# Decoder layer with a routed mixer: last expert's down products in one row, token ranks read with a selection mark, first expert's partial sums outside its weight slot

## The chip, the cores and the metric

The kernel runs on one core of one Trainium2 chip. The metric is device time of one execution in microseconds (us), from the first to the last instruction and what the runtime puts around them. Before the change the median of 3 runs is 339.26 us (338.2 to 341.36).

## What is computed

One decoder layer for 256 tokens of width 1024, all in float32. First come two attention groups (four heads of differential attention, eight heads of block-sparse attention) with one input and one output projection. Then follows a mixture of experts, and it alone is touched by the change:

```python
g_logits = t @ router_group                      # 256 tokens x 4 groups
g = argmax(g_logits)                             # one group for each token
e_logits = (t @ router_expert[g])                # 8 experts in that group
top_v, top_e = top_k(e_logits, 2)                # two experts for each token
weight = softmax(g_logits)[g] * softmax(top_v)
...
hid = silu(xc @ w_gate[e]) * (xc @ w_up[e])      # for each of 32 experts, hidden width 256
out = hid @ w_down[e]
y[token] += out * weight
```

Each expert has three weight matrices of 1 MB (w_gate, w_up, w_down), so the 32 experts read 96 MB, and the two projections 16 MB.

## The kernel before

**Stages.** The attention part fills the first 125 us or so. Then the residual is added, the router's logits are made (`routed`), and `select(c)` picks two experts for each token of the 128-token half c (c = 0, 1). The tokens of an expert get places in a slot table of 32 places (CAP): `select` multiplies the one-hot choices `oh` by the strict triangle `tri` (and by `ones` for the earlier half), which gives in PSUM, for every expert, how many chosen tokens stand before this one (`prk`). Two VectorE instructions (L569, L570) turn it into `R1`: the rank plus 1 where the token chose the expert, else 0. `places(g, c)` (L601) compares R1 with the numbers 1 to 32 (`iota1`) for the four experts of group g, which gives the gather matrix `Pm`, and scales it by the token's norm (`Ps`). Eight matmuls a half (L871) gather the tokens of the first four experts into `pgs`, `gathered` (L612) writes them to `xe`, and the experts begin.

**An expert.** `gate(e)` and `up(e)` (L668) multiply the expert's 32 gathered tokens by its weights, in 8 matmuls each, which lie in four column strips of the array and run four at a time (each is recorded as two passes, so 16 records). The results are partial sums over four strips. ScalarE (L678) and VectorE (L683) copy them to SBUF: **into the first 512 columns of the expert's own gate weight slot**, which is not read any more by then. One expert later `folded` (L688) transposes them on TensorE, adds the four strips, and makes the hidden values `hT`. Another expert later `down` (L706) multiplies by w_down. The outputs of four experts are gathered in `oG` and brought back to the tokens by `combine` (L741). For the last 8 experts each has its own way back: `moved` (L725, L726) copies the product from PSUM, and `spread` (L731) adds it to the tokens in 8 matmuls.

**Weights.** Units of 1 MB are loaded in the fixed order of their use, all on the queue of SyncE (SP), into 23 slots: 16 of a ring, others that open as earlier buffers end, and x2's place. Units 16 and 17 are w_gate and w_up of expert 0; the experts' units follow. `fill` issues a unit's transfer when its slot's last reader is done; the transfer waits for that reader's semaphore, and for the transfer eight issues earlier (eight completion semaphores in rotation). The ring's first refill by an expert's slot is unit 39 (w_up of expert 8), then 40 (w_down of expert 6) and 41. The last unit, 111 (w_down of expert 31), goes in pieces (`CUTS`): contraction half 0 whole (512 KB), half 1 in two pieces of 256 KB.

**Order.** TensorE runs the experts' matmuls in program order (`pe`). The places touched are `select`, `places`, `gate`, `weighted` (which allocated oG of the first group), the lines after the first expert, and the end: down(30), spread(29), half 0 of down(31), spread(30), two `warmed` matmuls (128x512 of zeros, whose result nobody reads), half 1 of down(31), and `last`: moved(31), spread(31), the copies to `res` and the output transfers.

Of the kernel before, what the change touches and what calls it, by code (L numbers as in the profile page):

```python
# [9 lines left out]
F32 = mybir.dt.float32  # L10
F32R = mybir.dt.float32r
BF16 = mybir.dt.bfloat16
# [3 lines left out]
ALU = mybir.AluOpType  # L16
# [19 lines left out]
LATE3_AT = 16 + SLOTS - 1  # L36
CUTS = ((0, 0, 1024), (1, 0, 512), (1, 512, 1024))
OVER_E, OVER_N = 12, 4
ROWS_Q = 4

A_COLS = {}
# [10 lines left out]
def hybrid_layer_kernel(ctx: ExitStack, tc: tile.TileContext, x, xt, w_in, w_out, w_gate, w_up, w_down, smalls, relb, out):  # L52
# [496 lines left out]
    def select(c):  # L549
        pl, d = pls[c], sel[c]  # L550
        gm, gi, pen = small("gm", 8), small("gi", 8, U32, xr), small("pen", 4, F32, xr)
        Lm, em, ei = small("Lm", E, F32, None, "t32", 3), small("em", 8), small("ei", 8, U32, xr)
        oh, mb = small("oh", 2 * E, BF16).rearrange("p (i e) -> p i e", i=2), small("mb", E, F32, None, "t32", 3)
        nc.vector.max(gm, pl[:, 32:40])
        nc.vector.max_index(gi, gm, pl[:, 32:40])
        nc.vector.tensor_tensor(pen, gi[:, 0:1].broadcast_to([P, 4]), col("iota")[:, 0:4], op=ALU.not_equal)
        nc.vector.scalar_tensor_tensor(
            Lm.rearrange("p (g e) -> p g e", g=4), pen.unsqueeze(2).broadcast_to([P, 4, 8]), -1.0e30,
            pl[:, 0:32].rearrange("p (g e) -> p g e", g=4), op0=ALU.mult, op1=ALU.add)
        nc.vector.max(em, Lm)  # L560
        nc.vector.max_index(ei, em, Lm)
        nc.vector.tensor_tensor(oh, ei[:, 0:2].unsqueeze(2).broadcast_to([P, 2, E]),
                                col("iota").unsqueeze(1).broadcast_to([P, 2, E]), op=ALU.is_equal)
        d["oh"] = oh
        prk = pl[:, 64 : 64 + E]
        in_order(*[lambda c2=c2, i=i: nc.tensor.matmul(
            prk, tri if c2 == c else ones, sel[c2]["oh"][:, i, :], start=c2 == 0 and i == 0, stop=c2 == c and i == 1)
            for c2 in range(c + 1) for i in range(2)])
        nc.vector.tensor_tensor(mb, oh[:, 0, :], oh[:, 1, :], op=ALU.add)  # L569
        nc.vector.scalar_tensor_tensor(R1[:, c, :], prk, 1.0, mb, op0=ALU.add, op1=ALU.mult)  # L570
        d.update(gm=gm, em=em)

# [29 lines left out]
    def places(g, c):  # L602
        p = ew.tile([P, G, CAP], F32, name="Pm", tag="Pm", bufs=2)
        r = R1[:, c, g * G : (g + 1) * G].unsqueeze(2).broadcast_to([P, G, CAP])
        it = col("iota1").unsqueeze(1).broadcast_to([P, G, CAP])
        nc.vector.tensor_tensor(p, r, it, op=ALU.is_equal)
        ps_ = ew.tile([P, G * CAP], F32, name="Ps", tag="Ps", bufs=2)
        state["ps"] = nc.vector.tensor_scalar(ps_, p.rearrange("p g s -> p (g s)"), rstd[:, c : c + 1], None, op0=ALU.mult)
        return p, ps_
# [35 lines left out]
    def weighted(st):  # L645
# [7 lines left out]
        st["pT"] = ex.tile([P, S], F32, name="pT", tag="pT")  # L653
        st["o"] = ex.tile([P, D], F32, name="oG", tag="oG")
        nc.scalar.activation(st["pT"], pt[:, :S], AF.Copy)
# [19 lines left out]
    def gate(e, st):  # L675
        t, pg = half(e, st, 0, place[e - 1][0] if e else None)
        st["parts"] = t
        nc.scalar.activation(*paired(t[:, :HID], pg), AF.Copy)  # L678
        return t
# [67 lines left out]

    def last(hT, dv, pd):
        res = spare("res").rearrange("p (c n) -> p c n", c=NC)
        for nh in range(2):  # L750
            down_product(hT, dv, pd, (1,), (2 * nh, 2 * nh + 1))
        moved(2 * G - 1, pd)
# [11 lines left out]
    def overflow():  # L764
        rv = nc.values_load(flag[0:1, 0:1], min_val=0, max_val=S)
        used["ring"] += [over_at - 1] * OVER_N
        with tc.If(rv > CAP):  # L767
# [20 lines left out]
            for c in range(NC):  # L788
                nc.vector.scalar_tensor_tensor(wo[:, c, :], R1[:, c, :], CAP + 0.5, W[:, c, :], op0=ALU.is_gt, op1=ALU.mult)
            with tc.For_i(0, E, 1) as ie:  # L790
# [64 lines left out]
    in_order(opened[0], *routed(1, 512, xTa), *turnb, opened[1])  # L855
    squared(1, 512, 256, ppa, 1)
    select(0)
    in_order(*routed(1, 768, xTb))
    squared(1, 768, 256, ppb, 2)
    pools["x2"] = x2.rearrange("p c n -> p (c n)")  # L860
# [23 lines left out]
    with tc.issue_after(state["ps"].ins):  # L884
        for c in range(NC):
            weights(c)
    pc = pls[1][:, 128 : 128 + E]
# [9 lines left out]
    for e in range(1, E):  # L897
# [37 lines left out]
        if 0 <= e - OVER_E - 1 < 2 * G:  # L935
            residual(*divmod(e - OVER_E - 1, G))
    down(*queue.pop(0), place[E - 1][0])
    spread(done.pop())
    dv = unit(place[E - 1][2]).rearrange("p (c n) -> p c n", c=2)
    pd = ps.tile([P, 512], F32, name="pd", tag="tr")  # L940
    down_product(hT, dv, pd, (0,), range(4))
    spread(2 * G - 2)
    warmed(2, "pp")
    last(hT, dv, pd)

# [18 lines left out]
def _layout(inputs):  # L964
# [8 lines left out]
    def rows(v):  # L973
# [11 lines left out]
        "g2p": a["norm2_g"][0].reshape(P, KC),  # L985
        "tri": (idx[:, None] < idx[None, :]).astype(np.float32),
        "iota": rows(np.arange(E, dtype=np.float32)),
        "iota1": rows(np.arange(1, CAP + 1, dtype=np.float32)),
        "router": np.concatenate(
# [29 lines left out]
```

## Time and profile before

| | us |
|---|---|
| median of 3 runs (lowest to highest) | 339.26 (338.2 to 341.36) |
| the profiled execution's own time | 340.07 |
| its span, first to last instruction | 337.8 |
| TensorE busy in the span | 317.0 (94%) |
| VectorE busy | 193.9 (57%) |
| ScalarE busy | 138.5 (41%) |
| GpSimd busy | 12.0 (4%) |
| mean granted clock of TensorE, of full speed | 0.98 |
| bytes moved | 123.20 MB, mean 365 GB/s |

Times within the span start at its first instruction. PE is TensorE's matmuls, PEld its weight loads, DVE VectorE, ACT ScalarE, POOL GpSimd, SP SyncE, whose only work is to issue transfers. A busy share is an average over stages with different limits. The granted clock is a share of 2.4 GHz: 1.00 is that level and 0.50 is 1.2 GHz. Some records of matmuls and of landings are missing.

### The profile page before, as it was taken

How to read it: one execution, taken by the hardware profiler on the slowest of the kernel's cores; microseconds unless marked ns; L12 is line 12 of the kernel's file. 1: busy time of each engine (PE TensorE's matmuls, PEld its weight loads, DVE VectorE, ACT ScalarE, POOL GpSimd, SP SyncE). 2: the span in 40 equal slices, each digit the busy share in tenths (PEclk: the TensorE clock that was granted, in tenths of full speed). 3: DMA queues.
4: the chain of work that ended last, by engine and by line, in shares of the span. 5: the costliest groups of instructions: out<-in, count | busy, mean ns of one | idle time of the engine just before them, and what ended most of it. 6: DMA issues, size and time to landing. Idle time of an engine off the chain costs nothing. (4 is left out here: it accounts for less than half of the span.)

```text
span 337.8 us, 7426 instructions
## 1 busy us (share of the span) xinstructions
PE 317.0 (94%) x2858; PEld 213.6 (63%) x2858; DVE 193.9 (57%) x601; ACT 138.5 (41%) x362; POOL 12.0 (4%) x20
## 2 busy tenths in 40 slices
PE   8889999999999998999999939999999999999971
PEld 4658877788777788575676714664665675575430
DVE  2767858878998657756454532355354466333302
ACT  4875667958786434324222221213213224212101
POOL 0100001000120131000000000000000000000000
PEclk9999999999999999999999996999999999999978
DMA  7999999999725896899999999999999999999923
GB/s 213 397 385 288 390 387 396 414 414 420 253 84 199 314 422 253 321 422 419 423 419 419 418 425 418 419 421 418 422 422 422 420 419 419 419 422 418 415 94 124
DMA packets 25544, 123.20 MB, mean 365 GB/s; under 512 B 2311, under 2 KB 3380, under 8 KB 13348
## 3 DMA queue, kind: packets, MB, share of 16 engines
q1 hardware_dynamic: 24772, 120.91, 89.4%
q0 software_dynamic: 304, 1.02, 1.0%
q10 hardware_dynamic: 432, 0.79, 0.7%
q8 instruction: 24, 0.39, 0.5%
q14 instruction: 12, 0.10, 0.1%
HBM read 121.64 MB, written 1.07 MB: 363 GB/s over the span
## 5 line engine op out<-in xcount | busy, mean ns | idle before, releaser
L668 PE MATMUL pgu<-u,xe 128*32 128x256 f32 x992 | 67.7, 391 | 6.4 <-PEq L767 5.5
L256 PE MATMUL pp<-hi,xh 128*128 128x512 f32 (+1 forms) x132 | 53.3, 405 | 2.2 <-ACT hi L245 2.2
L246 DVE TENSOR_TENSOR lo<-u,hi 128x512 fp32r<-128x512 f32 x63 | 43.1, 702 | 16.0 <-ACT hi L245 15.9
L256 PE MATMUL pp<-lo,xh 128*128 128x512 f32 (+1 forms) x132 | 51.5, 393 | 0.0
L256 PE MATMUL pp<-hi,xl 128*128 128x512 f32 (+1 forms) x132 | 51.5, 390 | 0.0
L668 PEld LDWEIGHTS pgu<-u,xe 128*32 128x32 f32 x992 | 28.9, 111 | 34.2 <-issue 13.2
L245 ACT ACTIVATE hi<-u 128x512 fp32r<-128x512 f32 x64 | 39.0, 626 | 19.0 <-PE pp L256 13.3
L720 ACT ACTIVATE oG<-pd 32x256 f32<-32x256 f32 x48 | 17.9, 374 | 56.9 <-PE pd L706 45.2
L706 PE MATMUL pd<-u,hT 128*32 128x256 f32 x496 | 34.0, 391 | 2.6 <-DMA u<-in_w_down_dram 2.4
L722 DVE COPY oG<-pd 32x256 f32<-32x256 f32 x48 | 20.3, 423 | 27.0 <-ACT oG L720 25.2
L256 PEld LDWEIGHTS pp<-hi,xh 128*128 128x128 f32 x132 | 25.0, 189 | 9.5 <-ACT hi L245 3.8
L256 PEld LDWEIGHTS pp<-lo,xh 128*128 128x128 f32 x132 | 24.8, 188 | 6.6 <-DVE rv L153 0.6
L256 PEld LDWEIGHTS pp<-hi,xl 128*128 128x128 f32 x132 | 24.9, 188 | 4.6
L624 PEld LDWEIGHTS pg<-Ps,x2q 128*128 128x128 f32 x224 | 25.5, 192 | 2.9 <-DVE gu L691 1.6
L624 PE MATMUL pg<-Ps,x2q 128*128 128x128 f32 x224 | 26.9, 278 | 0.0
L691 DVE TENSOR_REDUCE gu<-ptr 128x64 f32<-128x256 f32 x32 | 13.6, 425 | 21.2 <-PE ptr L688 20.8
L683 DVE COPY u<-pgu 128x256 f32<-128x256 f32 x31 | 13.2, 424 | 21.4 <-PE pgu L668 21.4
L706 PEld LDWEIGHTS pd<-u,hT 128*32 128x32 f32 x496 | 14.2, 111 | 15.1 <-issue 6.0
L741 PE MATMUL y<-oG,pT 128*128 128x256 f32 x96 | 21.7, 379 | 0.0
L688 PEld LDWEIGHTS ptr<-sm,u 128*128 128x128 f32 x124 | 13.3, 143 | 13.1 <-issue 10.2
L688 PE MATMUL ptr<-sm,u 128*128 128x128 f32 x124 | 20.8, 291 | 0.0
L678 ACT ACTIVATE u<-pgu 128x256 f32<-128x256 f32 x31 | 11.9, 383 | 20.4 <-PE pgu L668 19.3
(168 smaller groups left out, 359.9 us busy)
## 6 DMA issues: line engine op xcount, KB each, us to landing
u<-in_w_gate_dram SPq DMA_DIRECT2D x31, 1024.0 KB, 19.5
u<-in_w_up_dram SPq DMA_DIRECT2D x31, 1024.0 KB, 19.8
u<-in_w_down_dram SPq DMA_DIRECT2D x30, 1024.0 KB, 19.7
u<-in_w_in_dram SPq DMA_DIRECT2D x11, 1024.0 KB, 12.5
u<-in_w_out_dram SPq DMA_DIRECT2D x4, 1024.0 KB, 14.7
x<-in_x_dram SPq DMA_DIRECT2D x2, 512.0 KB, 10.9
x<-in_w_gate_dram SPq DMA_DIRECT2D x1, 1024.0 KB, 8.8
x<-in_w_down_dram SPq DMA_DIRECT2D x1, 1024.0 KB, 19.8
```

The costliest lines, as they stand in the source:

```text
L245: nc.scalar.activation(hi, raw, AF.Copy)
L246: (nc.gpsimd if u * 4 + k == 3 else nc.vector).tensor_tensor(lo, raw, hi.bitcast(F32), op=ALU.subtract)
L256: yield lambda a=a, w=w, kk=kk, i=i: nc.tensor.matmul(pp, a, w[:, cols], start=first and kk == 0 and i == 0, stop=last and kk == len(hls) ...
L624: pe(nc.tensor.matmul(pg[:, j * P : (j + 1) * P], x2q[:, c, q4 * 4 + j, :], st["P"][c][1], start=c == 0, stop=c == NC - 1))
L668: pe(nc.tensor.matmul(pg[q * CAP : (q + 1) * CAP, :HID], st["xe"][:, k, j0 : j0 + CAP], wv[:, k, :], start=r == 0, stop=r == KC // ROWS_Q ...
L683: nc.vector.tensor_copy(*paired(t[:, HID : 2 * HID], pg))
L688: pe(nc.tensor.transpose(pt[:, j * P : (j + 1) * P], t[:, j * P : (j + 1) * P], ident))
L691: nc.vector.tensor_reduce(gu[:, :2], parts[:, :2], axis=AX.X, op=ALU.add)
L706: pe(nc.tensor.matmul(pd[j * 32 : (j + 1) * 32, :256], hT[:, c, :], dv[:, c, j * 256 : (j + 1) * 256], start=c == 0, stop=c == 1, tile_pos ...
L720: nc.scalar.activation(dst, pd[j * 32 : (j + 1) * 32, :256], AF.Copy)
L722: nc.vector.tensor_copy(dst, pd[j * 32 : (j + 1) * 32, :256])
L741: pe(nc.tensor.matmul(y[j][:, c * 256 : c * 256 + 256], st["pT"][:, c * P : (c + 1) * P], st["o"][:, j * 256 : (j + 1) * 256], start=st["g ...
```

## The change

The change makes these edits.

- The triangle gets 512 (`SEL`) on its diagonal, so the product itself holds the rank plus 512 where the token chose the expert, and `iota1` runs from 512 to 543. The first group's places read this product in PSUM; the two instructions that made R1 are gone from `select`, and R1, which later groups use, is copied from PSUM after the first group's places, ahead of `weights`.
- Expert 0's partial sums go to oG, which is allocated at gate(0) now; `weighted` allocates it for later groups alone.
- At the end spread(29) and six `warmed` matmuls come ahead of down(30), all 8 products of down(31) follow down(30) directly, then spread(30) and `last`. The last unit's half 1 is one piece of 512 KB.
- `squared` stands two lines later in the source.

```diff
-CUTS = ((0, 0, 1024), (1, 0, 512), (1, 512, 1024))
+CUTS = ((0, 0, 1024), (1, 0, 1024))
...
+SEL = 512
...
-        nc.vector.tensor_tensor(mb, oh[:, 0, :], oh[:, 1, :], op=ALU.add)
-        nc.vector.scalar_tensor_tensor(R1[:, c, :], prk, 1.0, mb, op0=ALU.add, op1=ALU.mult)
-        d.update(gm=gm, em=em)
+        d.update(gm=gm, em=em, rank=prk)
...
-        r = R1[:, c, g * G : (g + 1) * G].unsqueeze(2).broadcast_to([P, G, CAP])
+        r = (R1[:, c] if g else sel[c]["rank"])[:, g * G : (g + 1) * G].unsqueeze(2).broadcast_to([P, G, CAP])
...
-        st["o"] = ex.tile([P, D], F32, name="oG", tag="oG")
+        if g:
+            st["o"] = ex.tile([P, D], F32, name="oG", tag="oG")
...
         t, pg = half(e, st, 0, place[e - 1][0] if e else None)
-        st["parts"] = t
+        if e == 0:
+            t = st["o"] = ex.tile([P, D], F32, name="oG", tag="oG")
...
-    def last(hT, dv, pd):
+    def last(pd):
         res = spare("res").rearrange("p (c n) -> p c n", c=NC)
-        for nh in range(2):
-            down_product(hT, dv, pd, (1,), (2 * nh, 2 * nh + 1))
         moved(2 * G - 1, pd)
...
-    squared(1, 512, 256, ppa, 1)
     select(0)
     in_order(*routed(1, 768, xTb))
+    squared(1, 512, 256, ppa, 1)
...
         for c in range(NC):
+            nc.vector.tensor_copy(R1[:, c, :], sel[c]["rank"])
             weights(c)
...
+    spread(done.pop())
+    warmed(6, "pp")
     down(*queue.pop(0), place[E - 1][0])
-    spread(done.pop())
     dv = unit(place[E - 1][2]).rearrange("p (c n) -> p c n", c=2)
     pd = ps.tile([P, 512], F32, name="pd", tag="tr")
-    down_product(hT, dv, pd, (0,), range(4))
+    down_product(hT, dv, pd, range(2), range(4))
     spread(2 * G - 2)
-    warmed(2, "pp")
-    last(hT, dv, pd)
+    last(pd)
...
-        "tri": (idx[:, None] < idx[None, :]).astype(np.float32),
+        "tri": (idx[:, None] < idx[None, :]).astype(np.float32) + SEL * np.eye(P, dtype=np.float32),
...
-        "iota1": rows(np.arange(1, CAP + 1, dtype=np.float32)),
+        "iota1": rows(np.arange(SEL, SEL + CAP, dtype=np.float32)),
```

In the built program the order of instructions moves at three places.

On VectorE, at the choice for the second half of the tokens, before. oh is the one-hot choice, mb and R_1581 (R1) are the two that go, pl is the PSUM bank with the rank:

```order
L561 MAX_INDEX ei<-em,Lm 128x8
L562 TENSOR_TENSOR oh<-ei,sm 128x64
L569 TENSOR_TENSOR mb<-oh 128x32
L570 SCALAR_TENSOR_TENSOR R_1581<-pl,mb 128x32
L606 TENSOR_TENSOR Pm<-R_1581,sm 128x128
L608 TENSOR_SCALAR Ps<-Pm,rstd 128x128
L586 SCALAR_TENSOR_TENSOR ngm<-gm,rstd 128x1
```

And after:

```order
L562 MAX_INDEX ei<-em,Lm 128x8
L563 TENSOR_TENSOR oh<-ei,sm 128x64
L605 TENSOR_TENSOR Pm<-pl,sm 128x128
L607 TENSOR_SCALAR Ps<-Pm,rstd 128x128
L885 COPY R_1581<-pl 128x32
L585 SCALAR_TENSOR_TENSOR ngm<-gm,rstd 128x1
L586 SCALAR_TENSOR_TENSOR ngm<-em,rstd 128x1
L885 COPY R_1581<-pl 128x32
```

Pm follows oh directly and reads PSUM, and two copies stand behind Ps. ScalarE's instructions stand in the same order before and after, so the moved `squared` moves nothing.

On SP's queue, at the first refills of the experts' slots, before. u_1784 is unit 39, u_1786 unit 40, u_1819 unit 41; in brackets stand the semaphores that each waits for (DMAHW: a transfer's completion):

```order
L140 DMA x_64<-in_w_gate_dram 128x2048 [waits PE_49,DMAHW5_49,Activation_49,Pool_49]
L140 DMA u_1784<-in_w_up_dram 128x2048 [waits DMAHW6_49,PE_49]
L140 DMA u_1786<-in_w_down_dram 128x2048 [waits DVE_49,DMAHW7_49,PE_49,Activation_49]
L140 DMA u_1819<-in_w_gate_dram 128x2048 [waits DMAHW0_49,PE_49]
L140 DMA u_1821<-in_w_up_dram 128x2048 [waits DVE_49,DMAHW1_49,PE_49,Activation_49]
```

And after (u_1781, u_1783, u_1816 and u_1818 are the same units 39 to 42):

```order
L141 DMA x_64<-in_w_gate_dram 128x2048 [waits PE_49,DMAHW5_49,Activation_49,Pool_49]
L141 DMA u_1781<-in_w_up_dram 128x2048 [waits DMAHW6_49,PE_49]
L141 DMA u_1783<-in_w_down_dram 128x2048 [waits DMAHW7_49,PE_49]
L141 DMA u_1816<-in_w_gate_dram 128x2048 [waits DMAHW0_49,PE_49]
L141 DMA u_1818<-in_w_up_dram 128x2048 [waits DVE_49,DMAHW1_49,PE_49,Activation_49]
```

The order is the same, the waits are not: unit 39 took the slot of unit 17 before and waited for the last matmul of up(0); it takes the slot of unit 16 now and waits for the last matmul of gate(0). Unit 40 took the slot of unit 16 and waited for the transposes of folded(0); it takes the slot of unit 17 now and waits for up(0).

On TensorE, at the end of the program, before. u_3384, u_3386 and u_3458 are w_down of experts 29, 30 and 31; an x8 of y is one spread:

```order
L688 MATMUL ptr<-sm,u_3324 128x128 x4
L706 MATMUL pd<-u_3384,hT 32x256 x8
L706 MATMUL pd<-u_3386,hT 32x256 x8
L731 MATMUL y<-oG,x_64 128x256 x8
L706 MATMUL pd<-u_3458,hT 32x256 x4
L731 MATMUL y<-oG,x_64 128x256 x8
L701 LDWEIGHTS zeros
L701 MATMUL warm<-zeros 128x512
L701 LDWEIGHTS zeros
L701 MATMUL warm<-zeros 128x512
L706 MATMUL pd<-u_3458,hT 32x256 x4
L731 MATMUL y<-oG,x_64 128x256 x8
```

And after (u_3380, u_3382 and u_3454 are the same three; four more pairs of the zeros stand where lines are left out):

```order
L689 MATMUL ptr<-sm,u_3320 128x128 x4
L707 MATMUL pd<-u_3380,hT 32x256 x8
L732 MATMUL y<-oG,x_64 128x256 x8
L702 LDWEIGHTS zeros
L702 MATMUL warm<-zeros 128x512
...
L702 LDWEIGHTS zeros
L702 MATMUL warm<-zeros 128x512
L707 MATMUL pd<-u_3382,hT 32x256 x8
L707 MATMUL pd<-u_3454,hT 32x256 x8
L732 MATMUL y<-oG,x_64 128x256 x16
```

The spread of expert 29 moved ahead of the wait for w_down of expert 30, and the spread of expert 30 behind the wait for the last piece of w_down of expert 31.

## Rows read from the trace of the kernel before

**Rows 1.** The page: the granted clock of TensorE in tenths of full speed, in 40 equal slices of the span (8.4 us each).

```profile
PEclk9999999999999999999999996999999999999978
```

**Rows 2.** The chain of waits that ended last, from 295 us on: start, length (both us), what.

```profile
302.35 20.98 DMA u<-in_w_down_dram
...
323.46 1.09 PE pd L706 x16
```

**Rows 3.** The waits of TensorE from 140 us to the end: who waited for what; us in total, times, longest.

```profile
PE pd L706 <- DMA u<-in_w_down_dram: 2.4, 1, 2.4
PE pgu L668 <- DMA u<-in_w_up_dram: 0.8, 1, 0.8
```

**Rows 4.** Busy time by stretch: the stretch, its length, busy us of PE, PEld, DVE, ACT, POOL (records in brackets), granted clock, DMA share, GB/s.

```profile
137.00:138.00 1.00, 1.00 (x19) 0.47 (x11) 0.75 (x5) 0.38 (x1) 0.00 (x0) 1.00 0.73 295
138.00:139.00 1.00, 1.00 (x22) 0.53 (x20) 0.94 (x5) 0.00 (x0) 0.00 (x0) 1.00 0.02 8
139.00:140.00 1.00, 1.00 (x16) 0.60 (x16) 0.46 (x3) 0.70 (x2) 0.00 (x0) 1.00 0.73 123
...
250.00:300.00 50.00, 48.98 (x557) 31.15 (x555) 26.50 (x78) 13.82 (x40) 0.00 (x0) 1.00 1.01 421
```

**Rows 5.** The timeline from 128 to 160 us: start, length, engine, line, operation, out<-in, count; in brackets the idle time before and what ended it.

```profile
129.96 0.33 SPq L140 DMA_DIRECT2D x<-in_w_gate_dram  x1
...
132.47 3.24 PE L871 MATMUL pp<-Ps,x2q 128*128 128x128 f32 x24
132.70 0.19 DVE L570 SCALAR_TENSOR_TENSOR R<-pl,mb 128x32 f32<-128x32 f32 x1
132.92 0.29 DVE L606 TENSOR_TENSOR Pm<-R,sm 128x128 f32<-128x128 f32 x1
133.25 0.29 DVE L608 TENSOR_SCALAR Ps<-Pm,rstd 128x128 f32<-128x128 f32 x1
...
133.66 1.86 PEld L871 LDWEIGHTS pp<-Ps,x2q 128*128 128x128 f32 x16 [0.24 <-issue]
...
135.75 0.76 DVE L612 TENSOR_TENSOR xe<-pp,sm 128x128 f32<-128x128 f32 x2
...
137.20 0.38 ACT L678 ACTIVATE u<-pgu 128x256 f32<-128x256 f32 x1 [2.22 <-PE pgu L668]
...
138.06 0.33 SPq L140 DMA_DIRECT2D u<-in_w_up_dram  x1
```

**Rows 6.** The page, transfers by issue: out<-in, engine, count, KB each, median us from issue to landing. The first is unit 38, the others are the pieces of the last unit.

```profile
x<-in_w_gate_dram SPq DMA_DIRECT2D x1, 1024.0 KB, 8.8
...
u<-in_w_down_dram SPq DMA_DIRECT2D x1, 512.0 KB, 19.8
u<-in_w_down_dram SPq DMA_DIRECT2D x2, 256.0 KB, 16.1
```

**Rows 7.** Line L140 from 137.9 to 138.4 us, which is unit 39 alone: its time to landing.

```profile
DMA to landing us min/median/max: 4.8/4.8/4.8
```

**Rows 8.** The waits of SP's queue in the whole span: total us, times, longest.

```profile
SPq L140 <- DMA u<-in_w_gate_dram: 38.6, 18, 3.4
...
SPq L140 <- PE ptr L688: 16.2, 10, 4.8
```

**Rows 9.** SP's timeline: the issues of the last unit's three pieces (the last of them 0.33 us before the end of the row).

```profile
304.82 5.25 SPq L143 DMA_DIRECT2D u<-in_w_down_dram  x3
```

**Rows 10.** The timeline from 318 us to the end, columns as in rows 5.

```profile
318.33 1.15 PE L731 MATMUL y<-oG,x 32*128 32x256 f32 x16
...
319.40 0.66 PE L688 MATMUL ptr<-sm,u 128*128 128x128 f32 x4
...
319.99 1.07 PE L706 MATMUL pd<-u,hT 128*32 128x256 f32 x16
...
321.44 0.29 DVE L726 COPY oG<-pd 128x128 f32<-128x128 f32 x1
...
324.49 2.09 PE L731 MATMUL y<-oG,x 32*128 32x256 f32 x16
...
326.51 1.08 PE L706 MATMUL pd<-u,hT 128*32 128x256 f32 x8
...
327.52 1.25 PE L731 MATMUL y<-oG,x 32*128 32x256 f32 x16
...
328.71 0.61 PE L701 MATMUL warm<-zeros 128*128 128x512 bf16 x2
...
329.24 0.64 PE L706 MATMUL pd<-u,hT 128*32 128x256 f32 x8
...
330.60 1.15 PE L731 MATMUL y<-oG,x 32*128 32x256 f32 x16 [0.72 <-DVE oG L726]
```

**Rows 11.** Busy time by stretch at the end, columns as in rows 4.

```profile
324.50:325.00 0.50, 0.50 (x7) 0.50 (x8) 0.09 (x1) 0.28 (x1) 0.00 (x0) 0.50 0.06 25
...
327.50:328.00 0.50, 0.50 (x12) 0.46 (x12) 0.00 (x0) 0.00 (x0) 0.00 (x0) 0.71 0.00 0
```

**Rows 12.** Line L701, the two matmuls of zeros near the end, and line L167, the 14 at the start of the program: duration in ns (least, median, most), first and last start in us.

```profile
L701 PE MATMUL warm<-zeros x2: 379/384/390, 328.7 to 328.9; 128*128 128x512 bf16 x2
...
L167 PE MATMUL warm<-zeros x14: 594/634/634, 1.0 to 6.5; 128*128 128x512 bf16 x14
```

More of the change, by code (lines that the diff above doesn't have):

```diff
@@ L552, in select @@
         Lm, em, ei = small("Lm", E, F32, None, "t32", 3), small("em", 8), small("ei", 8, U32, xr)
-        oh, mb = small("oh", 2 * E, BF16).rearrange("p (i e) -> p i e", i=2), small("mb", E, F32, None, "t32", 3)
+        oh = small("oh", 2 * E, BF16).rearrange("p (i e) -> p i e", i=2)
         nc.vector.max(gm, pl[:, 32:40])
@@ L788, in overflow @@
             for c in range(NC):
-                nc.vector.scalar_tensor_tensor(wo[:, c, :], R1[:, c, :], CAP + 0.5, W[:, c, :], op0=ALU.is_gt, op1=ALU.mult)
+                nc.vector.scalar_tensor_tensor(wo[:, c, :], R1[:, c, :], SEL + CAP - 0.5, W[:, c, :], op0=ALU.is_gt, op1=ALU.mult)
             with tc.For_i(0, E, 1) as ie:
```

## The prediction

> **What bounds the kernel now.** I read the chain of waits first, from its end. It runs back from the output over TensorE's last products to one transfer of 20.98 us, issued at 302.35 us, that ends in a product of w_down at 323.46 [rows 2]. That is the weights of expert 30. Twenty-one microseconds for 1 MB is no slow transfer: the busy time by stretch gives 421 GB/s over 250 to 300 us with the transfer engines' share at 1.01 [rows 4], so 1.049 MB takes 2.49 us, and eight transfers are under way at a time. SP's queue mostly waits for such a completion; the waits for a slot are fewer [rows 8]. So from about 140 us on the weight stream is never empty, and its end is set by its start.
>
> TensorE comes next: its list of waits from 140 us on has only 0.83 us for w_up of expert 31 and 2.40 us for w_down of expert 30 [rows 3] that a faster stream would remove. So TensorE lies some 3 us ahead of the weights at the end, and both have to come earlier for the kernel to end earlier.
>
> Two places are open. At the start of the stream the reader is to see a hole: the share falls to 0.73, 0.02 and 0.73 in the three microseconds from 137 [rows 4]. Unit 38 had been issued at 129.96 and the next issue is at 138.06 [rows 5]; they land 8.8 and 4.8 us later [rows 6, 7], at 138.76 and 142.86, so 4.10 us apart where 2.49 is the pace. The hole costs 1.61 us. At the end, the granted clock: it is 0.50 in the half microsecond from 324.5 and back to 0.71 in that from 327.5 [rows 11], so TensorE runs at 1.2 GHz for some 3 us, just after it has stood 2.40 us for weights. The page shows the last two slices below 9 and one more such slice, from 203 to 211 us [rows 1], which the stream hides.
>
> **The change part by part.**
>
> *Rank products.* In the second half of the tokens R1's instruction starts at 132.70 and the compare at 132.92 [rows 5]: 0.22 us leave the path, because the compare now starts when R1's did (the add for `mb` ended before the rank was there and counts for nothing). Ps would end 0.22 earlier, and the weight load behind it had waited 0.24 [rows 5], so the gather follows. The compare reads PSUM instead of SBUF, which no compare of this trace does; the nearest rows are 0.19 for R1's instruction, from PSUM, and 0.29 for the compare, from SBUF [rows 5], of which the first has a quarter of the elements; I add nothing, with 0.1 us either way. Two copies of 128x32 stand behind Ps at some 0.19 each, by R1's row. They delay ScalarE's exponentials, and nothing needs the weights W before the first combine. The first half gains nothing: its ranks wait for TensorE's router products. I take 0.2 us, between 0.1 and 0.24, for TensorE and for gate(0). The moved `squared` is 0, since no engine's order changes by it.
>
> *Partial sums outside the slot.* No instruction is added or removed; oG is allocated one stage earlier, over buffers whose readers are done. Unit 39 waits for gate(0) instead of up(0). ScalarE's copy of gate(0)'s result starts at 137.20 [rows 5], which bounds the moment from above; less the 0.2 it is 137.0, against an issue at 138.06: 1.05 us earlier. Unit 40 is issued when up(0) ends, near 137.9 instead of 139.88, and still behind 39. Does the stream use that? The lower bound is 0: a later wait for a slot, the longest of which are 4.8 us [rows 8], could empty the queue. The upper bound is the hole, 1.61. I take 1.05, because the share is 1.01 long after the last such wait [rows 4], and from the issue to the landing nothing else changes.
>
> Then w_up of expert 31 comes 1.05 earlier and takes TensorE's wait of 0.83 [rows 3]; with the 0.2 of the ranks, TensorE is 1.03 earlier at down(29).
>
> *The end, with the old arrivals.* down(29) ends at 321.06 [rows 10]. moved(29) ends with VectorE's copy at 321.73, so spread(29) starts at 321.79 where TensorE stood idle before. At full clock the next group follows a spread's start after 1.07 (318.33 to 319.40 [rows 10]), so at 322.86. Two matmuls of zeros take 0.53 from the first to the next group (328.71 to 329.24), and the pair of 0.61 less one of 0.384 [rows 10, 12] puts 0.23 between them: six take 0.53 + 4 x 0.23 = 1.45, until 324.31. The weights of down(30) are there at 323.46 by then. Eight products at full clock are 1.07 long, four are 0.64 [rows 10], so one half follows the other after 0.43: down(30) takes 0.86, half 0 of down(31) starts at 325.17, half 1 could start at 325.60. Its weights: the last piece is issued at 309.74 [rows 9] and lands after 16.1 [rows 6], 325.84, and a product started 0.13 after the landing in [rows 2]: 325.97. One piece of 512 KB instead of two of 256 KB I take at 0; the bytes are the same. Now TensorE has 0.43 of products and 0.22 of changeover (1.08 from products to the next group, less 0.86), spread(30) starts at 326.62 and runs 0.86 + 0.29, while moved(31) takes from the products' end at 326.61 the 0.72 that it took before (329.88 to 330.60): 327.33. spread(31) follows spread(30) at 327.48 and ends at 328.63. It ended at 331.75 [rows 10]. So 3.1 us.
>
> Half of this is the clock: spread(29) was 2.09 and not 1.15, half 0 of down(31) 1.08 and not 0.64, spread(30) 1.25 and not 1.15 [rows 10], together 1.5. TensorE's longest pause would now be the 0.73 for moved(29), so I take the full level.
>
> *Sum.* With the stream 1.05 and TensorE 1.03 earlier the weights still come last, and the end moves by 3.1 + 1.05 = 4.15. From the profiled execution's 340.07 that gives 335.9. It lies 0.8 above the median of 339.26, which would give 335.1. Since an execution in which the clock stays up has less to gain, I do not carry the whole 0.8 over and say 335.6.
>
> **The rivals.**
>
> *The early start is lost on the way.* The refills behind unit 42 still wait for TensorE (a wait of 4.8 us among them, rows 8), which is only 0.2 earlier. If the queue runs empty there once, or the slots become the pace, the 1.05 is gone and 3.1 is left: 337.0 from the profile, 336.5 on my scale. Against it speaks the share of 1.01.
>
> *The clock's fall was chance.* The pause of 2.40 us need not lower the clock in each execution. Where it does not, before has its last products 1.5 us earlier and the change is worth 4.15 - 1.5 = 2.65, under 1%: against a run of 338.6, after would be at the same 335.9. For it speaks that the three runs lie 3.2 us apart. The Trainium skill, "TensorE: Matmul & The Clock Gate", Part 1, says that the activity window runs freely and is not aligned with the program, so the place of a change of clock varies from run to run; by it, 2.65 would be the gain in a share of the pairs. This trace, with one pause of this length, cannot tell.
>
> *The new end falls to 1.2 GHz too.* The pause for moved(29) and that for the last weights (0.35) add up to 1.1 us; if they suffice, about the old 1.5 us are lost again: 337.1.
>
> *Slower: the six matmuls and a low clock from the first of them on.* If TensorE is down at spread(29) and stays down to the end, this block lies on the path and everything doubles: from 321.79, spread 2.0, six of zeros 6 x 0.46 = 2.8 (the 14 at the start lie 0.42 apart, rows 12), products 2 x 1.9, spreads 2 x 2.0: 334.4 against 331.75; less 1.05 it is 1.6 slower, 341.7. It decides once the clock is low ahead of spread(29), where it was 1.00 in the profile until after 324 [rows 1, 11]. More than 1% slower needs something that I don't see.
>
> *The change does not do what it says.* If the compare from PSUM is no faster, only 0.2 is lost.
>
> **How the numbers follow.** One per cent is 3.4 us, about what a measurement of this kernel tells from no change. The forecast gets 0.55, the lost start 0.14, the clock's chance 0.16, the clock low again 0.09, slower 0.06. Faster by over 1%: 0.8 of the forecast, as its 4.15 lies 0.75 above the bound and the unknowns of the start (0 to 1.61) reach to both sides, and 0.06 from the next two: 0.50. Slower by over 1%: 0.03. The rest, 0.47, is within 1%. The range starts from the most that the bounds give: with the hole filled TensorE's own path ends it, 3.1 + 0.37 (the wait for the last piece) + 1.03 = 4.5, from the median 334.8, and 0.8 for the runs' spread, 334.0. It ends with the lost start and the low clock together, 340.07 - 3.1 + 1.5 = 338.5.
>
> **What would show it.** Right: SP's issue of unit 39 near 137.0 with no second of share near 0.02, landings 1 us earlier to the end; w_up of expert 31 no wait; granted clock 1.00 in the last 15 us until the output; the last spread ending near 327.6, some 4.1 us before the old one. Wrong: the hole filled but the last piece landing near 325.8 as before; a wait of over 1 us at half 1 of down(31), which would mean that the path hangs on the last piece more than worked out; 0.50 in the clock's column; or R1's copies found in front of gathered's first row.

## The result, and the profile after

| | before | after |
|---|---|---|
| median of 13 runs each, us | 338.99 (337.51 to 341.36) | 336.46 (335.88 to 338.02) |
| ratio after to before | | 0.9926, 95% interval 0.9904 to 0.9949 |
| the profiled execution's own time, us | 340.07 | 335.96 |

So the change is worth 2.5 us of the median, by the interval 1.7 to 3.3. The time of 336.46 lies in the predicted range and 0.9 above the predicted 335.6. The gain is 0.74%, inside the one per cent within which the text counted a change as none; it had given 0.50 to a gain above one per cent and 0.47 to this. Between the two profiled executions the difference is 4.11, and the sum had 4.15. How both can be true is what most of the experiments are about. Three runs in the comparisons below (444.38 of the kernel before, 611.77 with the end alone, 342.33 with the ranks alone) were slow ones and are left out of the ratios, though not of the medians.

The granted clock by slices, on the page of the kernel after, answers to [rows 1]. The low slice in the middle is still there. Of the two low slices at the end only the last is left. It begins at 325.3, with the last products in it, but the clock is 1.00 to 329, which is behind them.

```profile
PEclk9999999999999999999999996999999999999997
```

The start of the weight stream after, to be read against [rows 5]: on DVE oh is the one-hot choice of the second half, pl the PSUM bank with the rank; on SPq the three issues are units 38, 39 and 40.

```profile
130.24 0.33 SPq L141 DMA_DIRECT2D x<-in_w_gate_dram  x1
...
132.44 0.23 DVE L563 TENSOR_TENSOR oh<-ei,sm 128x64 bf16<-128x64 uint32 x1
...
132.95 0.29 DVE L605 TENSOR_TENSOR Pm<-pl,sm 128x128 f32<-128x128 f32 x1 [0.29 <-PE pl L567]
133.28 0.29 DVE L607 TENSOR_SCALAR Ps<-Pm,rstd 128x128 f32<-128x128 f32 x1
133.48 0.18 DVE L885 COPY R<-pl 128x32 f32<-128x32 f32 x1
...
137.22 0.33 SPq L141 DMA_DIRECT2D u<-in_w_up_dram  x1
...
138.08 0.33 SPq L141 DMA_DIRECT2D u<-in_w_down_dram  x1
```

The compare that reads PSUM takes 0.29, as the one that read SBUF did, and R1's copy stands behind Ps. Unit 39 follows unit 38 after 6.98 us, where it was 8.10. Its time to landing is 5.0 where it was 4.8 [rows 7]:

```profile
DMA to landing us min/median/max: 5.0/5.0/5.0
```

Busy time by stretch after, columns as in [rows 4]: three microseconds at the start of the stream, and the two half microseconds of [rows 11].

```profile
137.00:138.00 1.00, 1.00 (x19) 0.46 (x10) 0.87 (x5) 0.38 (x1) 0.00 (x0) 1.00 0.85 352
138.00:139.00 1.00, 1.00 (x22) 0.55 (x20) 0.85 (x5) 0.00 (x0) 0.00 (x0) 1.00 0.98 147
139.00:140.00 1.00, 1.00 (x17) 0.58 (x13) 0.33 (x2) 0.68 (x2) 0.00 (x0) 1.00 0.86 352
...
324.50:325.00 0.50, 0.50 (x15) 0.03 (x5) 0.06 (x1) 0.28 (x1) 0.00 (x0) 1.00 0.00 0
327.50:328.00 0.50, 0.06 (x4) 0.00 (x0) 0.34 (x1) 0.42 (x2) 0.00 (x0) 1.00 0.00 0
```

The second with a share of 0.02 is gone, and the clock (the column ahead of the share) is 1.00 where it was 0.50 and 0.71.

TensorE's waits from 140 us on, against [rows 3]: that for w_down of expert 30 is gone, that for w_up of expert 31 is not.

```profile
PE pgu L668 <- DMA u<-in_w_up_dram: 0.8, 1, 0.8
PE ptr L641 <- ACT x L642: 0.8, 2, 0.5
PE y L732 <- DVE oG L727: 0.7, 1, 0.7
```

The chain of waits that ended last, from 296 us on, against [rows 2]: start, length, what.

```profile
296.38 20.05 DMA u<-in_w_up_dram
...
316.56 1.07 PE pgu L668 x16
...
323.56 2.06 PE pd L707 x32
```

It leaves the transfers at 316.42, with the weights for up(31); before, it left them at 323.33 (302.35 + 20.98), with those for down(30). From there on it names only work of TensorE and of the copies.

TensorE's end after, against [rows 10]: down(29), spread(29), the six matmuls of zeros, down(30) with down(31), a row of weight loads (PEld) inside it, and the last two spreads.

```profile
319.22 1.07 PE L707 MATMUL pd<-u,hT 128*32 128x256 f32 x16
...
321.01 1.15 PE L732 MATMUL y<-oG,x 32*128 32x256 f32 x16 [0.72 <-DVE oG L727]
...
322.09 1.47 PE L702 MATMUL warm<-zeros 128*128 128x512 bf16 x6
...
323.49 2.13 PE L707 MATMUL pd<-u,hT 128*32 128x256 f32 x32
...
324.98 0.16 PEld L707 LDWEIGHTS pd<-u,hT 128*32 128x32 f32 x8 [0.47 <-DMA u<-in_w_down_dram]
325.55 1.61 PEld L732 LDWEIGHTS y<-oG,x 32*128 32x128 f32 x32 [0.41 <-DVE oG L727]
325.55 2.01 PE L732 MATMUL y<-oG,x 32*128 32x256 f32 x32
```

The reader is to see the row at 324.98: weight loads for half 1 of down(31) wait 0.47 for the last piece. The chain, which goes by the products, hides this: the end of the stream still has its part in the end of the kernel. In this execution the wait costs little: from the first product of down(30) to the next spread it is 2.06, and 1.97 in a profile below in which nothing waits (old pieces). The last spread ends at 327.56, where it ended at 331.75.

### The profile page after: what moved, and what is told of

It reads as the page before. It is cut to its first block, busy times and chain, and to the rows that moved or that the text cites. A ratio compares the mean times of both kernels' runs of the same rounds, so it can differ in the third digit from the quotient of the medians.

```text
span 333.7 us, 7427 instructions
## 1 busy us (share of the span) xinstructions
PE 314.2 (94%) x2862; PEld 212.8 (64%) x2862; DVE 193.2 (58%) x599; ACT 138.6 (42%) x362; POOL 12.1 (4%) x20
## 3 DMA queue, kind: packets, MB, share of 16 engines
HBM read 121.64 MB, written 1.07 MB: 368 GB/s over the span
## 5 line engine op out<-in xcount | busy, mean ns | idle before, releaser
L707 PE MATMUL pd<-u,hT 128*32 128x256 f32 x496 | 32.9, 383 | 0.2 <-ACT x L642 0.2
L689 PE MATMUL ptr<-sm,u 128*128 128x128 f32 x120 | 20.1, 291 | 0.0
L742 PEld LDWEIGHTS y<-oG,pT 128*128 128x128 f32 x96 | 17.8, 190 | 2.2
## 6 DMA issues: line engine op xcount, KB each, us to landing
u<-in_w_up_dram SPq DMA_DIRECT2D x31, 1024.0 KB, 19.8
```

The source lines that it names most:

```text
L689: pe(nc.tensor.transpose(pt[:, j * P : (j + 1) * P], t[:, j * P : (j + 1) * P], ident))
L707: pe(nc.tensor.matmul(pd[j * 32 : (j + 1) * 32, :256], hT[:, c, :], dv[:, c, j * 256 : (j + 1) * 256], start=c == 0, stop=c == 1, tile_pos ...
L742: pe(nc.tensor.matmul(y[j][:, c * 256 : c * 256 + 256], st["pT"][:, c * P : (c + 1) * P], st["o"][:, j * 256 : (j + 1) * 256], start=st["g ...
```

## The experiments

**The parts one at a time.** The lines that decide in each, the other lines of that part as in the change:

```diff
# the end alone
+CUTS = ((0, 0, 1024), (1, 0, 1024))
...
+    spread(done.pop())
+    warmed(6, "pp")
     down(*queue.pop(0), place[E - 1][0])
...
+    down_product(hT, dv, pd, range(2), range(4))
     spread(2 * G - 2)
# the slot alone
+        if g:
+            st["o"] = ex.tile([P, D], F32, name="oG", tag="oG")
...
+        if e == 0:
+            t = st["o"] = ex.tile([P, D], F32, name="oG", tag="oG")
# the ranks alone
-        nc.vector.scalar_tensor_tensor(R1[:, c, :], prk, 1.0, mb, op0=ALU.add, op1=ALU.mult)
+        r = (R1[:, c] if g else sel[c]["rank"])[...]
```

The end alone:

> Only the end is changed (spread(29) and six matmuls of zeros ahead of down(30), down(31) whole, last piece 512 KB); weights issued as before. Theory A (three separate gains: end 1.5 to 1.6 at a full clock, start of the stream 0.7 to 0.9, ranks 0 to 0.2): 1.6 us faster than before in the medians (337.3), 3.1 against an execution in which the clock falls; the profile shows granted clock 1.00 until the output and the last spread ending 0.7 to 1.0 later than in the changed kernel, near 328.4. Rival B (the end does it all, the early start is lost): 2.5 faster, 336.5. Rival C (the clock falls in each execution of before): 3.1 faster, 335.9.

Measured: 337.72, ratio 0.9954 (0.9926 to 0.9982), so 1.6 us faster, as theory A had it. Its profile has the granted clock at 1.00 to the output, but its last spread ends at 329.32 and not near 328.4: counted from the issue of unit 38 that is 198.94, where the changed kernel has 197.32. The stream was late in this execution, with w_gate of expert 31 waited for by 1.42 us.

The slot alone:

> Only the first expert's partial sums go to oG; ranks and end as before. Theory A: unit 39 issued 0.7 to 0.9 earlier, landings that much earlier to the end, the old end starts as much earlier: 0.8 us faster (338.2). Rival B (early start lost at a later wait for a slot): landings of the last units as before, 0.0 (339.0). Whether the clock falls in the old end stays open here: the profile shows it once.

Measured: 337.02, ratio 0.9948 (0.9918 to 0.9978), 1.8 us by the ratio, more than the 0.8 expected. Rival B, the early start lost on the way, does not fit its profile: down(30) starts 191.62 us after the issue of unit 38, where five profiles of before have 192.17 or more. SP's timeline of this kernel, units 38 and 39:

```profile
130.34 0.33 SPq L140 DMA_DIRECT2D x<-in_w_gate_dram  x1
137.57 0.33 SPq L140 DMA_DIRECT2D u<-in_w_up_dram  x1
```

The ranks alone:

> Only the ranks are read with the mark in PSUM. Theory A: from oh to Ps of the second half 0.84 us instead of 1.11, gate(0) ends 0.2 earlier, unit 39 behind up(0) 0.2 earlier, so 0.2 us faster at most (338.8). Rival: the time in front of the first product is TensorE's own (router products, gather), 0.0. Neither is told apart by the times; the issue of unit 39 in the profile tells it.

Measured: 337.88, ratio 0.9964 (0.9934 to 0.9994), 1.2 us and more than the 0.2 expected, at the edge of what can be told from nothing. With the run of 342.33 counted, whose mean granted clock of 0.976 is like that of the executions below with a low clock at their end, the gain of the mean falls from 0.9 to 0.5. The same two issues:

```profile
130.24 0.33 SPq L141 DMA_DIRECT2D x<-in_w_gate_dram  x1
138.08 0.33 SPq L141 DMA_DIRECT2D u<-in_w_up_dram  x1
```

From one issue to the other it is 8.10 us in the kernel before, 7.84 with the ranks alone, 7.23 with the slot alone, 6.98 after. So the two parts are worth 0.26 and 0.87, and together 1.12. At this place they add up. The times add up worse: 1.6, 1.8 and 1.2 from the three ratios make over 4.5, where the whole change gives 2.5. But each of the three is uncertain by 1.0, and all are held against the same 35 runs of before, so this alone is weak.

Ranks and slot together, with the old end (the edits of both, `CUTS`, `last` and the last lines as before):

> Ranks and partial sums as in the changed kernel, the end as in the kernel before. Theory A (gains of the start and of the end add up, the clock falls by chance in a part of the runs): 1.0 us faster than before where the clock stands (336.5 to 337.0 the lowest runs), about 338.2 in the median, with some runs 1.5 to 3 higher; the stream's end about 1.4 us nearer to the issue of unit 38 than in before. Rival F (the single parts don't add up, since each of them also avoids a slow phase of before): median 336.8 to 337.2, as the slot alone.

Measured: 337.05, ratio 0.9938 (0.9916 to 0.9961), so 2.1 us. Its lowest run is 336.72; the lowest of all runs are 337.27 before, 336.49 with the end alone and 335.88 after. Read so, start and end are worth 0.55 and 0.78 and together 1.39, which adds up, though the least of a few runs is a rough number. By the ratios, 2.1 and 1.6 make 3.7 against 2.5, a difference that the intervals still allow. The median of 337.05 lies where rival F had put it, and not at theory A's 338.2. A possible reason, which no run here proves, is that each part also takes away some of the later executions of before, which can go only once; the next runs show what these are.

**Why the executions of before differ.** The kernel before was profiled four more times, without an edit.

> The kernel before once more, for its profile. Theory A (the fall of the clock in the last products is chance; by the mean granted clock of its 35 timed runs some 8 have it for certain): most likely 1.00 in the last products, spread(31) ending 328.5 to 330.5, the pause for w_down of expert 30 between 1.2 and 2.4 us. Rival C (it falls whenever the pause is there): 0.50 after the pause, spread(31) ending near 331.7.

> The kernel before a third time, for its profile; expectations as for the second.

> The kernel before a fourth time, for its profile. Three profiles of it so far end their last spread at 331.75, 330.81 and 329.00, with TensorE's pause for w_down of expert 30 at 2.40, 1.39 and 1.22 us; only the first has the low clock behind it. Theory A2 (two things vary from execution to execution: when the weights of expert 30 land, by about 1 us, and, behind a pause of over 2 us, the clock): a pause near 1.2 to 1.4 goes with 1.00 and a time of 337.3 to 339.2, one near 2.4 with 0.50 and 340 to 341. Rival G (the fall has nothing to do with the length of the pause): 0.50 behind a pause near 1.2, or 1.00 behind one near 2.4.

> The kernel before a fifth time, for its profile; expectations as for the fourth.

The five profiles of one and the same kernel (the first is that of the rows):

| own time | unit 38 issued | transfer of w_down(30) | pause for it | granted clock behind it | start of down(30) to end of last spread | last spread ends, after issue of 38 |
|---|---|---|---|---|---|---|
| 340.07 | 129.96 | 20.98 | 2.40 | 0.50 | 8.29 | 201.79 |
| 339.14 | 130.51 | 20.88 | 1.39 | 1.00 | 6.77 | 200.31 |
| 337.33 | 130.07 | 19.81 | 1.22 | 1.00 | 6.77 | 198.94 |
| 337.75 | 130.33 | 19.82 | 1.26 | 1.00 | 6.77 | 199.09 |
| 341.07 | 130.35 | 20.78 | 2.21 | 0.50 | 8.28 | 202.41 |

TensorE's timeline of the third of them, down(30) and the last spread, and a half microsecond of its busy time by stretch:

```profile
322.24 1.07 PE L706 MATMUL pd<-u,hT 128*32 128x256 f32 x16 [1.22 <-DMA u<-in_w_down_dram]
...
327.86 1.15 PE L731 MATMUL y<-oG,x 32*128 32x256 f32 x16 [0.72 <-DVE oG L726]
```

```profile
324.50:325.00 0.50, 0.50 (x12) 0.12 (x6) 0.00 (x0) 0.00 (x0) 0.00 (x0) 1.00 0.06 12
```

And of the fifth, the same places:

```profile
324.48 1.93 PE L706 MATMUL pd<-u,hT 128*32 128x256 f32 x16 [2.21 <-DMA u<-in_w_down_dram]
326.34 1.79 PE L731 MATMUL y<-oG,x 32*128 32x256 f32 x16
...
331.61 1.15 PE L731 MATMUL y<-oG,x 32*128 32x256 f32 x16 [0.72 <-DVE oG L726]
```

```profile
325.00:326.00 1.00, 1.00 (x16) 0.33 (x8) 0.00 (x0) 0.00 (x0) 0.00 (x0) 0.50 0.09 35
```

The pauses fall into two groups, and only the long ones had the low clock behind them: in the fifth execution down(30) is then 1.93 long instead of 1.07, in the first the spread behind it is 2.09 instead of 1.15. So rival C, that the clock falls behind every pause, is out; rival G, that the length of the pause has nothing to do with it, found no case in five. The second execution ended 0.3 later than the 330.5 to which theory A had put it.

Two things vary, then, and the table parts them. The one is the landing of w_down(30): its product starts 192.17 to 194.13 us after the issue of unit 38. Its transfer took 19.8 in two executions and 20.8 to 21.0 in three, and in the fifth it was also issued later, 173.2 after unit 38 where the others have 172.2 to 172.5. From the chains of waits, the second profile and the third:

```profile
303.02 20.88 DMA u<-in_w_down_dram
```

```profile
302.29 19.81 DMA u<-in_w_down_dram
```

The other is the clock, which costs 1.5 from the start of down(30) to the end. The first and the second execution are the plainest pair: down(30) starts 193.50 and 193.54 after the issue of unit 38, so its weights were equally late. In the second, TensorE had already waited for the weights of down(29), its pause ahead of down(30) was 1.39 and not 2.40, and the clock stayed up.

The timed runs show roughly how often the clock is low. The two profiles with the low clock have a mean granted clock of 0.980 and 0.979, the other three 0.984 to 0.987. Of 65 timed runs of before in these comparisons 15 have 0.981 or less, with a median of 340.5; the other 50 have 338.75. So by this sign, which five profiles support, a low clock in the tail goes with 1.75 us and is seen in about a quarter of the executions. It does not explain the whole spread: four of the 50 took over 340 us too.

TensorE's waits in the second profile, a late arrival without a low clock: w_gate and w_up of expert 31 and w_down of experts 29 and 30 are waited for.

```profile
315.51 1.07 PE L668 MATMUL pgu<-u,xe 128*32 128x256 f32 x16 [0.98 <-DMA u<-in_w_gate_dram]
...
317.98 1.07 PE L668 MATMUL pgu<-u,xe 128*32 128x256 f32 x16 [0.81 <-DMA u<-in_w_up_dram]
...
321.58 1.07 PE L706 MATMUL pd<-u,hT 128*32 128x256 f32 x16 [0.87 <-DMA u<-in_w_down_dram]
...
324.05 1.07 PE L706 MATMUL pd<-u,hT 128*32 128x256 f32 x16 [1.39 <-DMA u<-in_w_down_dram]
```

**Zeros in the pause, old order.**

```diff
+    warmed(6, "pp")
     down(*queue.pop(0), place[E - 1][0])
     spread(done.pop())
```

> The kernel before with six matmuls of zeros put into TensorE's pause ahead of down(30), order otherwise old. The zeros end 0.9 us before the weights of expert 30 land, so they cost nothing. Theory A (the clock falls in the old end in a part of the executions, and this costs 1.5 there): the upper half of before's spread goes away, all runs between 337.3 and 338.5, the median 0.5 to 1.5 lower; granted clock 1.00 at the end, last spread ending near 330.2. Rival C (it falls in each): median 1.5 lower, 337.5, and the spread stays. Rival D (the fall isn't due to the pause): clock 0.50 in the last products again, time as before.

Measured: 338.89, ratio 0.9994 (0.9967 to 1.0021). No run is above 340.0 and none has a mean clock under 0.982, so the upper end of the spread went away, which fits theory A, though 12 runs are few. The other two expectations of theory A failed: the runs lie between 338.01 and 340.0, not 337.3 and 338.5, and the median did not come down by 0.5 to 1.5. The profile is as expected, with the clock at 1.00 and the last spread ending at 330.55, 6.77 after the start of down(30):

```profile
321.37 1.07 PE L706 MATMUL pd<-u,hT 128*32 128x256 f32 x16
322.38 1.47 PE L701 MATMUL warm<-zeros 128*128 128x512 bf16 x6
323.78 1.07 PE L706 MATMUL pd<-u,hT 128*32 128x256 f32 x16
```

From the start of down(29) to that of down(30) it is 2.41. In the two executions of before with the short pause it was 2.29 and 2.33, so the zeros would delay those by about 0.1. A gain of 1.5 in a quarter of the executions would be 0.4 in the mean, which this interval, from 1.1 faster to 0.7 slower, can't tell from nothing. Keeping the clock up by itself is thus no measurable gain here, and a small one is not ruled out.

**The new end without its zeros.**

```diff
     spread(done.pop())
-    warmed(6, "pp")
     down(*queue.pop(0), place[E - 1][0])
```

> The changed kernel without its six matmuls of zeros; spread(29) still ahead of down(30). TensorE then stands idle from the end of spread(29) until the weights of expert 30 land, an estimated 0.5 to 1.5 us behind the 0.72 us for moved(29). Theory A (what keeps the clock up in the tail is that the one pause of 2.4 us is gone): time as with the zeros, 336.5, granted clock 1.00 until the output in the profile. Rival E (the zeros are needed): 0.50 in the last products in part or all of the executions, 337.0 to 338.0, and runs above 338.0.

Measured: 336.40, ratio to before 0.9921 (0.9897 to 0.9945), the same as with them, and the six runs span only 336.1 to 336.77. Theory A, though the pause is not where it was expected: nothing is waited for ahead of down(30), and TensorE waits 1.09 for the last piece, inside the block:

```profile
322.54 1.50 PE L707 MATMUL pd<-u,hT 128*32 128x256 f32 x24
325.13 0.64 PE L707 MATMUL pd<-u,hT 128*32 128x256 f32 x8 [1.09 <-DMA u<-in_w_down_dram]
325.70 2.01 PE L732 MATMUL y<-oG,x 32*128 32x256 f32 x32
```

The zeros fill a wait that costs nothing, and nothing here needs them.

**The changed kernel again, and with the old pieces.** No edit in the one; in the other `CUTS = ((0, 0, 1024), (1, 0, 512), (1, 512, 1024))`.

> The changed kernel once more, for its profile. Theory A2: in its end a landing that varies by 1 us is met by the zeros and by the block of sixteen products, so TensorE's wait there is 0 to 0.6 and the last spread ends 327.4 to 328.3 at a granted clock of 1.00. Rival: a wait over 1 us ahead of down(30) or inside down(31), or 0.50 behind it, with a time above 337.5.

Measured: 335.95. The last spread ends 197.27 us after the issue of unit 38, against 197.32 in the first profile and 197.29 without the zeros: in these profiles the 3.5 us over which the end of before moved are gone. They are executions of 336.1 and less; what lies behind the runs of after that go up to 338.02, none of them profiled, stays open. Half 1 of down(31) again waits for its weights:

```profile
324.98 0.16 PEld L707 LDWEIGHTS pd<-u,hT 128*32 128x32 f32 x8 [0.38 <-DMA u<-in_w_down_dram]
```

> The changed kernel with half 1 of the last unit in two pieces of 256 KB instead of one of 512 KB, all else the same. Theory A (the bytes are the same, the sixteen products wait for both pieces anyway): 336.5, within 0.3 of the changed kernel. Rival (a smaller row of 2 KB instead of 4 KB, or one more issue, costs landing time): 0.3 to 1.0 slower.

Measured: 336.33, ratio to before 0.9919 (0.9891 to 0.9947). One piece or two is the same, as theory A had it; the last spread ends 197.34 after the issue of unit 38. No version tried beats the changed kernel by more than the measurement can tell.

## Why the prediction was right, and where not

**Right, nearly to the tenth, for the execution that was profiled.** The start was put at 1.05 and is 1.12, measured from the issue of unit 38 to that of 39. The ranks were put at 0.2, and from oh to Ps it is 0.84 us instead of 1.11. The compare from PSUM is no dearer, as taken. From the last piece to the end of the last spread the prediction had 325.97 to 328.63, 2.66; it is 324.98 to 327.56, 2.58. Six matmuls of zeros were put at 1.45 to the next product and take 1.40. The wait at half 1 was put at 0.35 of TensorE; the weight loads wait 0.47, of which the products lose about 0.1. The clock is 1.00 to the output. The last spread was to end near 327.6. Some of this closeness is luck: unit 38 was issued 0.28 later in the execution after than in the one before, and the times in the text are not counted from it. Counted so, the last spread ends 4.47 earlier, against the 4.15 of the sum.

**A sign of being wrong that came and cost nothing.** R1's copies were not to stand in front of gathered's first row. They do, at 133.48 and 133.72 against 134.88. But VectorE still stands idle for 0.49 between them, waiting for ScalarE, and counted from the issue of unit 38 the row at 134.88 starts 0.25 earlier than before.

**Wrong: that w_up of expert 31 would be waited for no more, and TensorE gain 1.03 by that.** The wait is 0.82 as before, and 0.81 to 0.83 in all profiles of before. The profile that waits for w_gate of expert 31 as well shows why: gate(31) and up(31) start 2.47 apart, one transfer's pace, and TensorE has 1.66 of work for that time (1.07 of gate(31) and 0.59 of the transposes). When the stream comes earlier, gate(31) moves with it, and the same wait opens behind. In two other profiles gate(31) and up(31) start less than that apart, 2.11 with the slot alone and 1.57 with the old pieces, and the wait is 0.47 and none; by this reckoning TensorE came to gate(31) there when its weights had been in place for a while. TensorE's down(29) starts 0.77 earlier because w_up of expert 31 starts its products 0.76 earlier (317.32 to 316.56), by the stream alone. Counted from the issue of unit 38 it is 1.05, so the predicted 1.03 came out, by luck and for another reason. The step did no harm to the sum, since the end hung on the last piece.

**Wrong: what the sum was held against.** The 3.1 for the end were worked out from one execution with the pause of 2.40 and the clock of 0.50. The step that failed is the carrying over: 335.6 was set between 335.9 from that execution and 335.1 from the median, with the whole 4.15 taken off either way, though the text itself said that an execution whose clock stays up has less to gain. The term that was too large for the median is the 3.1. The late landing and the low clock are both in it, and neither is there in each execution: the landing was late in 3 of 5 profiles, the clock low in 2, and by the mean clock in 15 of 65 runs. Against the 197.32 of the changed kernel the five executions of before end 4.5, 3.0, 1.6, 1.8 and 5.1 later, counted from the issue of unit 38. With an early landing and the full clock the whole change is thus worth 1.6 to 1.8, of which 1.12 is the start. The rival named for it, that the clock's fall was chance, was given 0.16 and priced at 2.65; the change measures 2.5, and that the two lie so close is in part luck, since no profile of before has this gain. Against the 50 runs with the higher mean clock it is 338.75 - 336.46 = 2.3, against the 15 it is 4.0, near the 4.11 of the two profiles. That rival was itself too simple: it took the pause as given and the clock as the thing that varies, and in five profiles the length of the pause varied too, with the clock low behind the two long ones. The Trainium skill's rule that the prediction quoted for it ("TensorE: Matmul & The Clock Gate", Part 1, a window not aligned with the program) would let the place of the fall vary; here the low clock was there exactly where the pause was long, and whether a long pause can pass without it no run shows.

**The other rivals.** The early start was not lost: the last piece came 1.0 earlier than the 325.97 worked out for the old arrivals. The new end did not fall to the low clock in any profile, and no run of after has a mean clock under 0.984. The slower case, the zeros at a low clock, did not come up; its sum has 0.46 for each of the zeros where the rows that it names give 0.42, which is 0.2 us in all.

**Open.** Why w_down of expert 30 lands up to 2 us later in some executions, with the same issues ahead of it: its transfer takes 1.0 to 1.2 longer there, and in one case it is issued later as well, but no run shows the cause. And why the start alone, with a pause of 1.24 still in its one profile, has no run above 338.34 in nine: by the share of before two would be expected, so it may be luck.

## What to carry to other kernels

One profile is one draw: before a sum is made from its waits, look at the spread of the timed runs (here 3.2 us over three of them), and if it is as large as the gain in question, price the change once with the wait as shown and once without it. A wait that stays as long as it was when everything ahead of it moves can be the pace of the stream, and then it is no gap to be filled. An order that meets a late transfer with work that is ready anyway wins most in the executions in which it is late, so its gain shows in the spread as well as in the median.

## What the runs showed of the hardware

The end of the stream runs thinner than the rest. The view of transfers of the kernel after, 319 to 325 us in 40 slices: the busy share in tenths, what was moved, and the instruction loads in this stretch (packets, MB, share of sixteen engines):

```profile
DMA  9898988676666665455665594430001001000000
GB/s 464 355 464 355 410 328 355 273 300 246 246 246 273 273 246 246 191 246 219 246 246 218 246 328 191 191 137 27 27 0 27 0 0 27 0 27 0 0 0 0
...
q8 instruction: 1, 0.02, 1.1%
```

The share falls to about 0.6 at 320 and to nearly nothing only after 323, where it was 1.01 from 250 to 300. The view gives the mean of the sixteen engines, so it does not tell whether some of them stand idle for these 3 us or all of them in part. One instruction load in this stretch takes 1.1% of sixteen engines' 6 us, which is 1.06 us if one engine carries it. That such loads make the late landings of before is a guess that was not tried, and their number does not speak for it: from 296 to 329 us the profile of before with an early landing (own time 337.33) has four of them, as have two of the late ones.
